# Grouping x loads and output stores of an eight-expert MoE feed-forward, and one buffer size for w2, on one Trainium2 core

## The chip, the cores and the metric

One of the eight cores of a Trainium2 (trn2) chip runs the kernel. The metric is the device time of one execution in microseconds (us); lower is better. The number for a kernel is the median of its runs.

## The reference

```python
def reference(x, w1, w2):
    h = np.matmul(x, w1)
    h = np.maximum(h, 0)
    return np.matmul(h, w2).astype(np.float32)
```

There are 8 experts. x is 8 x 256 x 512, w1 is 8 x 512 x 2048, w2 is 8 x 2048 x 512, the output 8 x 256 x 512, all in fp32 in HBM. Each expert's 256 rows pass through two dense layers with a ReLU between them. The weights are 4 MB per expert and layer, 64 MB in all; x and the output are 0.5 MB per expert.

## The kernel before

The kernel computes in bf16 with fp32 accumulation. Nearly every load converts fp32 to bf16 on the way, in the DMA itself; such loads are issued from POOL (GpSimd), all on one queue (q0 in the profile). Only x of experts 0 and 1 is loaded as fp32 from SP, and cast on VectorE (`load_x_first`, L60 to L64).

Per expert there are three steps. `prepare` (L104) transposes x on TensorE, 8 blocks of 128 x 128, and VectorE copies the result to SBUF. `layer1` (L117) makes the 16 blocks of 128 hidden units, two at a time: 4 matmuls of 128 x 256 for each block (L125), then a ReLU on ScalarE (L132). `layer2` (L139) accumulates two output tiles of 128 x 512 over the 16 rows k of the hidden dimension: 32 matmuls (L148); for experts 6 and 7, whose w2 comes in pieces, with k as the outer loop (L144), so that a piece can be used as it lands. The finished tiles are copied to SBUF (L157, L159).

A "row" of w2 is here one k: 128 partitions x 512 columns, 256 KB read and 128 KB written. A w2 of one piece has 16 rows. `PIECES` (L53) splits expert 6 into 8, 4, 4 and expert 7 into 4, 4, 3, 2, 1, 1, 1 rows, and each size has a buffer pool of its own (`BUFS`, L54; three buffers for the whole w2). w1 has 4 buffers, x in bf16 has 4, the output 5.

The order on TensorE and POOL is written out by hand (L166); the other engines' order follows from the data. `loads` (L89 to L94) holds the loads in their order: for each expert x of the next one, w1, w2; at the end w1 of expert 7 goes ahead of w2 of expert 6. `issue` (L96) takes loads from its front as long as they are allowed at this point of the loop. In the loop over experts (L172) POOL issues loads two to three experts ahead, then the store of the expert before (L175), while TensorE runs layer 1 of expert e, the transposes of e + 1, layer 2 of e. In the last turn layer 1 of expert 7 is put ahead of layer 2 of expert 6 (L178). Experts 4, 5 and 6 (`DEFER`, L56) are stored after all loads (L181). Expert 7's two output tiles are stored by SP and ACT, each as soon as it is copied (L160 to L162).

A load waits on POOL until its buffer is free, and also until the transfer eight places earlier on POOL's queue has landed, since that one's semaphore is used again. Everything behind it in POOL's order waits too.

Of the kernel before, what the change touches and what calls it, by code (L numbers as in the profile page):

```python
# [9 lines left out]
FP32 = mybir.dt.float32  # L10
BF16 = mybir.dt.bfloat16


@with_exitstack
def kernel(
    ctx: ExitStack,
    tc: tile.TileContext,
    x: bass.AP,
    w1: bass.AP,
    w2: bass.AP,  # L20
    out: bass.AP,
):
    nc = tc.nc
    P = 128
    E, C, H = x.shape
    F = w1.shape[2]
    MC = C // P
    K1 = H // P
    K2 = F // P

    x_v = x.rearrange("e (p mo) k -> e p (mo k)", mo=MC)
    out_v = out.rearrange("e (p mo) k -> e p (mo k)", mo=MC)
    w1_v = w1.rearrange("e (p ko) n -> e p (ko n)", ko=K1)
    w2_v = w2.rearrange("e (p j) n -> e p (j n)", p=P)

    const = ctx.enter_context(tc.tile_pool(name="const", bufs=1))
    x_pool = ctx.enter_context(tc.tile_pool(name="x_pool", bufs=2))
    xb_pool = ctx.enter_context(tc.tile_pool(name="xb_pool", bufs=4))  # L40
    xT_pool = ctx.enter_context(tc.tile_pool(name="xT_pool", bufs=2))
    w1_pool = ctx.enter_context(tc.tile_pool(name="w1_pool", bufs=4))
    w2_pool = ctx.enter_context(tc.tile_pool(name="w2_pool", bufs=1))
    hT_pool = ctx.enter_context(tc.tile_pool(name="hT_pool", bufs=2))
    out_pool = ctx.enter_context(tc.tile_pool(name="out_pool", bufs=5))
    psum_t = ctx.enter_context(tc.tile_pool(name="psum_t", bufs=1, space=bass.MemoryType.PSUM))
    psum_h = ctx.enter_context(tc.tile_pool(name="psum_h", bufs=3, space=bass.MemoryType.PSUM))
    psum_o = ctx.enter_context(tc.tile_pool(name="psum_o", bufs=4, space=bass.MemoryType.PSUM))

    identity = const.tile([P, P], BF16, name="identity")  # L50


    PIECES = {E - 2: [8, 4, 4], E - 1: [4, 4, 3, 2, 1, 1, 1]}  # L53
    BUFS = {16: 3, 8: 1, 4: 4, 3: 1, 2: 1, 1: 3}  # L54

    DEFER = (E - 4, E - 3, E - 2)  # L56

    xbs, w1s, w2s, outs = {}, {}, {}, {}

    def load_x_first(e):  # L60
        t = x_pool.tile([P, MC * H], FP32, name="x_sb")
        nc.sync.dma_start(t[:], x_v[e])
        xbs[e] = xb_pool.tile([P, MC, P, K1], BF16, name="xb")
        nc.vector.tensor_copy(xbs[e][:].rearrange("p m q k -> p (m q k)"), t[:])  # L64

    def load_x(e):
        xbs[e] = xb_pool.tile([P, MC, P, K1], BF16, name="xb")
        nc.gpsimd.dma_start(xbs[e][:].rearrange("p m q k -> p (m q k)"), x_v[e])  # L68

    def load_w1(e):  # L70
        w1s[e] = w1_pool.tile([P, K1 * F], BF16, name="w1_sb")
        nc.gpsimd.dma_start(w1s[e][:], w1_v[e])  # L72

    def load_w2(e):
        w2s[e] = []
        k = 0
        for n in PIECES.get(e, [16]):
            c = w2_pool.tile([P, n * H], BF16, name=f"w2_{n}", bufs=BUFS[n])
            nc.gpsimd.dma_start(c[:], w2_v[e, :, k * H:(k + n) * H])  # L79
            for q in range(n):  # L80
                w2s[e].append(c[:, q * H:(q + 1) * H])
            k += n

    def store(e):
        nc.gpsimd.dma_start(out_v[e], outs[e][:].rearrange("p m h -> p (m h)"))  # L85

    loads = []  # L89
    for e in range(E):  # L90
        if e + 1 < E and e >= 1:
            loads.append((load_x, e + 1))
        loads += [(load_w1, e), (load_w2, e)]
    loads[-3], loads[-2] = loads[-2], loads[-3]  # L94

    def issue(upto):  # L96
        while loads:
            f, e = loads[0]
            if (f, e) not in upto:
                break  # L100
            loads.pop(0)
            f(e)

    def prepare(e):  # L104
        xb = xbs[e]
        xt_ps = psum_t.tile([P, K1, MC, P], BF16, name="xt_ps")
        for ko in range(K1):
            for mo in range(MC):
                nc.tensor.transpose(xt_ps[:, ko, mo, :], xb[:, mo, :, ko], identity[:])  # L109
        xT = xT_pool.tile([P, K1, C], BF16, name="xT")  # L110
        nc.vector.tensor_copy(  # L111
            xT[:].rearrange("p k c -> p (k c)"),
            xt_ps[:].rearrange("p k m q -> p (k m q)"),
        )
        return xT

    def layer1(e, xT):  # L117
        w1_r = w1s[e][:].rearrange("p (ko q j) -> p ko q j", ko=K1, j=K2)
        hT = hT_pool.tile([P, K2, C], BF16, name="hT")
        for pr in range(K2 // 2):  # L120
            h_ps = psum_h.tile([P, 2, C], FP32, name="h_ps")
            for s in range(2):
                j = pr * 2 + s
                for ko in range(K1):
                    nc.tensor.matmul(  # L125
                        h_ps[:, s, :],
                        w1_r[:, ko, :, j],
                        xT[:, ko, :],
                        start=(ko == 0),
                        stop=(ko == K1 - 1),  # L130
                    )
            nc.scalar.activation(  # L132
                hT[:, pr * 2:pr * 2 + 2, :].rearrange("p a c -> p (a c)"),
                h_ps[:].rearrange("p a c -> p (a c)"),
                mybir.ActivationFunctionType.Relu,
            )
        return hT

    def layer2(e, hT):  # L139
        last = e == E - 1  # L140
        out_sb = outs[e] = out_pool.tile([P, MC, H], FP32, name="out_sb")
        o_ps = [psum_o.tile([P, H], FP32, name="o_ps") for _ in range(MC)]
        if e in PIECES:
            order = [(k, m) for k in range(K2) for m in range(MC)]  # L144
        else:
            order = [(k, m) for m in range(MC) for k in range(K2)]
        for k, m in order:
            nc.tensor.matmul(  # L148
                o_ps[m][:],
                hT[:, k, m * P:(m + 1) * P],  # L150
                w2s[e][k],
                start=(k == 0),
                stop=(k == K2 - 1),
            )
            if k == K2 - 1:
                if last and m == 1:
                    nc.scalar.copy(out_sb[:, m, :], o_ps[m][:])  # L157
                else:
                    nc.vector.tensor_copy(out_sb[:, m, :], o_ps[m][:])  # L159
                if last:  # L160
                    eng = nc.scalar if m == 1 else nc.sync
                    eng.dma_start(out_v[e, :, m * H:(m + 1) * H], out_sb[:, m, :])  # L162

    load_x_first(0)
    load_x_first(1)
    with tc.manual_schedule(engines={mybir.EngineType.PE, mybir.EngineType.Pool}):  # L166
        f, e = loads.pop(0)
        f(e)
        make_identity(nc, identity)
        issue([(load_w2, 0), (load_x, 2), (load_w1, 1), (load_w2, 1), (load_x, 3), (load_w1, 2)])  # L170
        xT = prepare(0)
        for e in range(E - 1):  # L172
            issue([(load_w2, e + 2), (load_x, e + 4), (load_w1, e + 3), (load_w1, E - 1), (load_w2, e + 1)])
            if e > 0 and e - 1 not in DEFER:
                store(e - 1)  # L175
            hT = layer1(e, xT)
            xT = prepare(e + 1)
            if e == E - 2:  # L178
                hT_last = layer1(E - 1, xT)
            layer2(e, hT)  # L180
        for e in DEFER:  # L181
            store(e)
        layer2(E - 1, hT_last)


# [1 line left out]
_INS = ['x', 'w1', 'w2']  # L187
_OUTS = [((8, 256, 512), 'float32')]
# [25 lines left out]
```

## Time and profile before

| | us |
|---|---|
| median of 8 runs | 184.25 (183.96 to 184.78) |
| the profiled execution | 184.25 |
| its span | 182.5 |
| busy: PE, PEld | 131.6, 92.2 |
| busy: ACT, POOL, DVE | 40.1, 20.8, 17.1 |
| mean granted TensorE clock | 0.931 |

The span is the part of the execution that the trace shows; 1.75 us lie around it. A profile page gives busy time by engine, then the span in 40 slices with a digit for each engine (tenths busy), then the DMA queues, then the chain of work that ended last, then groups of instructions with what ended the idle time before each, and last the DMA issues with the KB written and the time from issue to landing. In the names, `w_sb` is w1, `w` is w2 and `xb` is x in bf16. The trace behind the page can be asked for one line's instructions, for waits, and for any window of time. In a window "DMA share" is the mean busy share of the 16 DMA engines; it can pass 1 because packets overlap.

### The profile page before, as it was taken

To read this page: it belongs to the slowest core of one execution; us is meant where nothing else is said; L and a number is where in the kernel's file an instruction comes from. 1 tells how busy PE (TensorE), PEld (TensorE's weight loads), DVE (VectorE), ACT (ScalarE), POOL (GpSimd) and SP (SyncE) were. 2 spreads that over 40 slices of the span, in tenths; PEclk is the share of its full clock that TensorE was granted. 3 is DMA by queue.
4 is the path that set the end of the run, shared out by engine and by line. 5 is a ranking of instruction groups with operands and counts; after the bars stand their busy time and mean duration, and the time that the engine had idled before them with its cause. 6 is when DMAs were issued, how large, how long until landed. Compare 5 with 4: busy or idle time off the path is not lost.

```text
span 182.5 us, 1871 instructions
## 1 busy us (share of the span) xinstructions
PE 131.6 (72%) x824; PEld 92.2 (51%) x832; DVE 17.1 (9%) x25; ACT 40.1 (22%) x66; POOL 20.8 (11%) x43
## 2 busy tenths in 40 slices
PE   0205999199974999289970999929887498999860
PEld 0104884079423874079430795328732397964320
DVE  1200011100120011100130001200102001001010
ACT  2000450026101440026100252004600064630010
POOL 7401010110201011010200202011020101122200
PEclk9999999969999799969998589996999789999998
DMA  7999999999999999999999999999998999999993
GB/s 257 199 226 215 201 219 226 219 208 192 243 226 201 208 226 226 205 205 209 247 183 259 198 205 240 230 248 215 221 235 190 215 228 260 204 259 228 204 350 140
DMA packets 5911, 40.48 MB, mean 222 GB/s; under 512 B 656, under 2 KB 1040, under 8 KB 3984
## 3 DMA queue, kind: packets, MB, share of 16 engines
q0 software_dynamic: 5328, 38.80, 97.4%
q1 hardware_dynamic: 432, 1.31, 1.9%
q10 hardware_dynamic: 144, 0.26, 0.4%
q8 instruction: 6, 0.10, 0.2%
q14 instruction: 1, 0.01, 0.0%
HBM read 71.30 MB, written 4.19 MB: 414 GB/s over the span
## 4 chain that ended last, share of the span: by engine, by line
DMA 62%; another core or an unknown queue 25%; POOL 4%; PE 3%; issue 3%; ACT 0%; POOLq 0%
DMA w_sb<-in_w_dram 24%; DMA xb<-in_x_dram 24%; DMA w<-in_w_dram 15%; PE o_ps L148 3%; POOL w L79 1%; POOL xb L68 1%; POOL w_sb L72 1%; POOL out_dram L85 1%; ACT out_sb L157 0%; POOL identity masks.py:199 0%; POOL identity masks.py:197 0%; POOLq L79 0%; POOLq L85 0%; POOLq L198 0%
## 5 line engine op out<-in xcount | busy, mean ns | idle before, releaser
L125 PE MATMUL h_ps<-xT,w_sb 128*128 128x256 bf16 x512 | 71.1, 310 | 36.1 <-DMA w_sb<-in_w_dram 35.2
L125 PEld LDWEIGHTS <-w_sb 128*128 128x128 bf16 x512 | 63.3, 150 | 45.4 <-DMA w_sb<-in_w_dram 39.4
L132 ACT ACTIVATE hT<-h_ps 128x512 bf16<-128x512 f32 x64 | 38.2, 597 | 121.6 <-PE h_ps L125 121.6
L148 PE MATMUL o_ps<-w,hT 128*128 128x512 bf16 x248 | 56.6, 379 | 4.2 <-DMA w<-in_w_dram 3.8
L148 PEld LDWEIGHTS <-hT 128*128 128x128 bf16 x256 | 24.9, 98 | 33.7 <-issue 5.5
L79 POOL DMA_DIRECT2D w<-in_w_dram x16 | 8.7, 542 | 63.0 <-DMA w_sb<-in_w_dram 36.6
L159 DVE COPY out_sb<-o_ps 128x512 f32<-128x512 f32 x15 | 10.3, 691 | 58.1 <-PE o_ps L148 58.1
L111 DVE COPY xT<-xt_ps 128x1024 bf16<-128x1024 bf16 x8 | 5.5, 691 | 97.4 <-PE xt_ps L109 97.4
L109 PE MATMUL xt_ps<-identity,xb 128*128 128x128 bf16 x64 | 5.3, 230 | 4.7 <-DVE xb L64 4.7
L72 POOL DMA_DIRECT2D w_sb<-in_w_dram x8 | 4.6, 574 | 31.1 <-DMA w<-in_w_dram 17.8
L85 POOL DMA_DIRECT2D out_dram<-out_sb x7 | 3.8, 537 | 33.8 <-DMA w<-in_w_dram 11.3
L109 PEld LDWEIGHTS <-xb 128*128 128x128 bf16 x64 | 4.7, 117 | 4.7 <-DVE xb L64 4.7
L68 POOL DMA_DIRECT2D xb<-in_x_dram x6 | 3.2, 532 | 22.8 <-DMA w_sb<-in_w_dram 13.4
L157 ACT COPY out_sb<-o_ps 128x512 f32<-128x512 f32 x1 | 0.6, 586 | 14.7 <-PE o_ps L148 14.7
L64 DVE CAST xb<-x_sb 128x1024 bf16<-128x1024 f32 x2 | 1.4, 694 | 4.5 <-DMA x_sb<-in_x_dram 4.5
L132 ACT ACT_TABLE_LOAD x1 | 1.3, 1283 | 0.7 <-PEq L198 0.7
masks.py:199 POOL TENSOR_SCALAR_AFFINE_SELECT identity<-identity 128x128 bf16<-128x128 bf16 x1 | 0.3, 289 | 0.1
masks.py:197 POOL MEMSET identity<- 128x128 bf16 x1 | 0.2, 225 | 0.0
L198 POOL MEMSET const-float32-0.0<- 128x1 f32 x1 | 0.1, 99 | 0.2 <-issue 0.2
L198 POOL MEMSET const-bfloat16-1.0<- 128x1 bf16 x1 | 0.1, 102 | 0.0
L198 POOL MEMSET const-uint8-127<- 128x1 uint8 x1 | 0.1, 102 | 0.0
L198 POOL MEMSET const-float32-1.0<- 128x1 f32 x1 | 0.1, 99 | 0.0
## 6 DMA issues: line engine op xcount, KB each, us to landing
w_sb<-in_w_dram POOLq DMA_DIRECT2D x8, 2048.0 KB, 51.9
w<-in_w_dram POOLq DMA_DIRECT2D x6, 2048.0 KB, 49.0
out_dram<-out_sb POOLq DMA_DIRECT2D x7, 512.0 KB, 32.4
w<-in_w_dram POOLq DMA_DIRECT2D x4, 512.0 KB, 36.8
xb<-in_x_dram POOLq DMA_DIRECT2D x6, 256.0 KB, 45.0
x_sb<-in_x_dram SPq DMA_DIRECT2D x2, 512.0 KB, 3.6
w<-in_w_dram POOLq DMA_DIRECT2D x1, 1024.0 KB, 47.1
w<-in_w_dram POOLq DMA_DIRECT2D x1, 384.0 KB, 18.8
```

The source lines that it names most:

```text
L64: nc.vector.tensor_copy(xbs[e][:].rearrange("p m q k -> p (m q k)"), t[:])
L68: nc.gpsimd.dma_start(xbs[e][:].rearrange("p m q k -> p (m q k)"), x_v[e])
L72: nc.gpsimd.dma_start(w1s[e][:], w1_v[e])
L79: nc.gpsimd.dma_start(c[:], w2_v[e, :, k * H:(k + n) * H])
L85: nc.gpsimd.dma_start(out_v[e], outs[e][:].rearrange("p m h -> p (m h)"))
L109: nc.tensor.transpose(xt_ps[:, ko, mo, :], xb[:, mo, :, ko], identity[:])
L111: nc.vector.tensor_copy(xT[:].rearrange("p k c -> p (k c)"), xt_ps[:].rearrange("p k m q -> p (k m q)"),)
L125: nc.tensor.matmul(h_ps[:, s, :], w1_r[:, ko, :, j], xT[:, ko, :], start=(ko == 0), stop=(ko == K1 - 1),)
L132: nc.scalar.activation(hT[:, pr * 2:pr * 2 + 2, :].rearrange("p a c -> p (a c)"), h_ps[:].rearrange("p a c -> p (a c)"), mybir.ActivationF ...
L148: nc.tensor.matmul(o_ps[m][:], hT[:, k, m * P:(m + 1) * P], w2s[e][k], start=(k == 0), stop=(k == K2 - 1),)
L157: nc.scalar.copy(out_sb[:, m, :], o_ps[m][:])
L159: nc.vector.tensor_copy(out_sb[:, m, :], o_ps[m][:])
```

## The change

- x of experts 2 to 7 is loaded in pairs (2, 3), (4, 5), (6, 7), one DMA each; there are two pair buffers.
- Outputs are stored in groups, one DMA each: (0, 1), (2, 3), and (4, 5, 6) after all loads. Expert 7 is stored as before. Each group has an output tile of its own, so none is used twice.
- w2 has one buffer size, of 16 rows, four of them. Pieces are slices of one such tile: expert 6 in 8, 8 and expert 7 in 4, 4, 4, 2, 2.
- Ahead of the loop the first two loads (w1 and w2 of expert 0) are taken singly, and the identity for the transposes is made twice.

```diff
-    PIECES = {E - 2: [8, 4, 4], E - 1: [4, 4, 3, 2, 1, 1, 1]}
-    BUFS = {16: 3, 8: 1, 4: 4, 3: 1, 2: 1, 1: 3}
-    DEFER = (E - 4, E - 3, E - 2)
+    PIECES = {E - 2: [8, 8], E - 1: [4, 4, 4, 2, 2]}
+    GROUPS = [(0, 1), (2, 3), (4, 5, 6), (7,)]
+    GROUP = {e: g for g in GROUPS for e in g}
+    DEFER = GROUPS[-2]
+    X_GROUPS = [(2, 3), (4, 5), (6, 7)]
...
-    def load_x(e):
-        xbs[e] = xb_pool.tile([P, MC, P, K1], BF16, name="xb")
-        nc.gpsimd.dma_start(xbs[e][:].rearrange("p m q k -> p (m q k)"), x_v[e])
+    def load_x(g):
+        t = xb_pool.tile([P, 2, MC, P, K1], BF16, name="xb2")
+        nc.gpsimd.dma_start(
+            t[:].rearrange("p e m q k -> p e (m q k)"), xg_v[:, g[0]:g[0] + 2, :]
+        )
+        for i, e in enumerate(g):
+            xbs[e] = t[:, i]
...
-        w2s[e] = []
+        w2s[e] = t = w2_pool.tile([P, K2 * H], BF16, name="w2_sb")
         k = 0
-        for n in PIECES.get(e, [16]):
-            c = w2_pool.tile([P, n * H], BF16, name=f"w2_{n}", bufs=BUFS[n])
-            nc.gpsimd.dma_start(c[:], w2_v[e, :, k * H:(k + n) * H])
-            for q in range(n):
-                w2s[e].append(c[:, q * H:(q + 1) * H])
+        for n in PIECES.get(e, [K2]):
+            nc.gpsimd.dma_start(t[:, k * H:(k + n) * H], w2_v[e, :, k * H:(k + n) * H])
             k += n
...
-    def store(e):
-        nc.gpsimd.dma_start(out_v[e], outs[e][:].rearrange("p m h -> p (m h)"))
+    def store(g):
+        nc.gpsimd.dma_start(
+            og_v[:, g[0]:g[-1] + 1, :], outs[g][:].rearrange("p e m h -> p e (m h)")
+        )
...
         f, e = loads.pop(0)
         f(e)
         make_identity(nc, identity)
-        issue([(load_w2, 0), (load_x, 2), (load_w1, 1), (load_w2, 1), (load_x, 3), (load_w1, 2)])
+        f, e = loads.pop(0)
+        f(e)
+        make_identity(nc, identity)
+        issue([(load_w2, 0), (load_x, X_GROUPS[0]), (load_w1, 1), (load_w2, 1), (load_w1, 2)])
         xT = prepare(0)
         for e in range(E - 1):
-            issue([(load_w2, e + 2), (load_x, e + 4), (load_w1, e + 3), (load_w1, E - 1), (load_w2, e + 1)])
-            if e > 0 and e - 1 not in DEFER:
-                store(e - 1)
+            issue(
+                [(load_w2, e + 2), (load_w1, e + 3), (load_w1, E - 1), (load_w2, e + 1)]
+                + [(load_x, g) for g in X_GROUPS if g[0] <= e + 4]
+            )
+            for g in GROUPS[:-2]:
+                if g[-1] == e - 1:
+                    store(g)
...
-        for e in DEFER:
-            store(e)
+        store(DEFER)
         layer2(E - 1, hT_last)
```

`xg_v` and `og_v` are x and out seen as "p e (mo k)": for each partition, the experts, and for each expert 4 KB.

## The prediction

> **What bounds the kernel now.** I first read the page's part 2 (slices) and part 3 (queues), then the landings of single transfers, then the chain of waits, and last the final 12 us in short windows.
>
> ```profile
> PE 131.6 (72%) x824; PEld 92.2 (51%) x832; DVE 17.1 (9%) x25; ACT 40.1 (22%) x66; POOL 20.8 (11%) x43
> ...
> DMA  7999999999999999999999999999998999999993
> ...
> q0 software_dynamic: 5328, 38.80, 97.4%
> ...
> HBM read 71.30 MB, written 4.19 MB: 414 GB/s over the span
> ```
>
> TensorE is busy 72% of the span, but the DMA row is 9 in all slices except the first, one in the middle and the last, and POOL's queue q0 alone fills 97.4%. The kernel is a stream of bytes. The wait list says the same: layer 1 waits 35.2 us for w1.
>
> Next, whether that stream ever runs dry. POOL issues each transfer long before it lands:
>
> ```profile
> w_sb<-in_w_dram POOLq DMA_DIRECT2D x8, 2048.0 KB, 51.9
> w<-in_w_dram POOLq DMA_DIRECT2D x6, 2048.0 KB, 49.0
> out_dram<-out_sb POOLq DMA_DIRECT2D x7, 512.0 KB, 32.4
> ```
>
> The last number is us from issue to landing; the KB are those written (bf16), so a weight load reads 4 MB. With some 50 us between issue and landing there are always several transfers queued, and POOL's own waits, most of them for the landing of the transfer eight places earlier, cost nothing.
>
> Adding issue and time to landing for single transfers gives the pace: w1 of expert 2 lands at 57.4, w2 of expert 2 at 67.1, x of expert 4 at 68.3, w1 of expert 3 at 78.0. So 9.7 us for a full weight, 1.25 for a 0.5 MB x. One place is out of line: w1 of expert 4 lands at 100.2, 11.3 us after x of expert 5 (88.9), with the DMA share at 1.01 in 88 to 101. The page does not say why.
>
> The end is the chain's last part, and the windows (length, busy us of PE, PEld, DVE, ACT, POOL, clock, DMA share, GB/s):
>
> ```profile
> 144.18 26.60 DMA w<-in_w_dram
> 170.78 0.04 issue
> 170.82 1.89 PE o_ps L148 x8
> 172.71 0.01 issue
> 172.72 0.81 PE o_ps L148 x3
> 173.52 0.05 issue
> 173.57 2.32 PE o_ps L148 x10
> 175.90 0.04 issue
> 175.94 0.61 PE o_ps L148 x2
> 176.54 0.02 issue
> 176.57 0.59 ACT out_sb L157
> ```
>
> ```profile
> 176.00:177.00 1.00, 0.53 (x2) 0.04 (x1) 0.65 (x1) 0.43 (x1) 0.00 (x0) 1.00 1.06 434
> 177.00:178.00 1.00, 0.00 (x0) 0.00 (x0) 0.04 (x1) 0.15 (x1) 0.00 (x0) 1.00 0.58 234
> 178.00:179.00 1.00, 0.00 (x0) 0.00 (x0) 0.00 (x0) 0.00 (x0) 0.00 (x0) 1.00 1.03 397
> ```
>
> The pieces of the last w2 land at 168.3, 170.8, 172.7, 173.9, 174.6, 175.1, 175.9. The last two matmuls run right after, the copies, and the two final stores are issued at 177.07 (SP) and 177.18 (ACT). Behind the last piece in q0 are the three deferred stores, landing at 177.2, 178.4, 179.7; the final stores land at 180.3 and 181.0, that is 0.6 and 1.3 later. Each is 256 KB, 0.6 at the stream's pace, so on the slowest of the 16 DMA engines they stood behind the deferred stores. At 177 to 178 the DMA share is 0.58: other engines were already empty. So bytes set the end, with the chain of matmul, copy and store close behind.
>
> **What the Trainium skill says.** "DMA: Bandwidth & Descriptors", section "Anatomy of one DMA", gives a transfer a fixed 2.0 us, mostly completion latency, and says that DMA engines wait on no semaphore, the issuing sequencer does. The trace agrees with the second. The first is latency, not occupancy: one-row pieces land 0.5 to 0.8 us apart. "Rules for kernel authors" of the same page advises one large transfer for many small ones, and counts those under 64 KB as mostly overhead; the smallest here writes 128 KB, and the last five pieces together lie 5% above the pace (below), so this trace leaves little to win.
>
> **The change part by part**, against the profiled execution (184.25 us, span 182.5, 1.75 around it; the runs' median is also 184.25).
>
> *Bytes.* None removed: weights, x and outputs are the same. With a stream that never dries, only the cost per transfer and the two ends can change.
>
> *Fewer transfers.* q0 goes from 37 to 27: x 6 to 3, stores 7 to 3, pieces of w2 10 to 7. What one costs beyond its bytes: a full weight has 16 rows in 9.7 us, 0.606 a row. The last five pieces of the last w2 (3, 2, 1, 1, 1: 8 rows) took 175.9 - 170.8 = 5.1 against 4.85, so 0.05 each. An x or a store is worth two rows, 1.21, and took 1.25 to 1.29: 0.04 to 0.08 each. What is not shown is whether this belongs to the transfer or to its 128 rows. For the pieces both go, so 3 x 0.05 = 0.15 is saved in either case. For the seven merged x and stores the rows stay: between 0 and 7 x 0.08 = 0.55. I take 0.04 each, 0.28. Sum 0.43, bounds 0.15 and 0.7. All of it lies in the one stream, so it counts in full as long as the stream sets the end.
>
> *Shape.* The grouped x and stores step over experts inside one transfer. No transfer of that shape is in this trace; they are 3 x 2.5, 2 x 2.5 and 3.8, some 16 us. The descriptor's run per expert is the same 4 KB of fp32, so I price it at nothing, from -0.2 to +0.8 (5% of 16).
>
> *The last pieces: 4, 4, 4, 2, 2.* Matmuls go at 7.07 / 31 = 0.23 each. Before, the last piece freed two; now four. From the second piece's landing T1: before, the third piece landed at T1 + 1.9, and PE, hardly idle since, ended at T1 + 5.76. After, the third piece has four rows and lands at T1 + 2.45; 16 matmuls from there end at T1 + 2.45 + 3.67 + about 0.1 = T1 + 6.2. So the final stores are issued about 0.45 later relative to T1, T1 itself 0.2 earlier. Is it covered? The last piece lands at T1 + 4.95, three stores follow in 3.7 to 3.8, the final ones in 1.25: T1 + 9.95. By the chain: issue at T1 + 6.75 (SP) and 6.85 (ACT); a first transfer on the idle SP queue at the start took about 3.2 from issue for 512 KB, so 2.0 beyond its 1.2; the ACT store then ends near T1 + 6.85 + 2.0 + 0.6, or + 1.2 behind SP's: 9.45 to 10.05. The bytes still last as long or longer. I take 0; without cover it costs 0.45.
>
> *Deferred stores as one.* It waits for the copies of expert 6. Before, the first of the three went at 166.5; those copies end at 169.2, so the one is issued there. Nothing but POOL's end is queued behind it, and the engines reach it only after the last piece (175.7). Over 5 us of cover: 0.
>
> *Second identity, w2 of expert 0 issued singly.* 0.23 + 0.29 on POOL, with a wait perhaps 0.6, ahead of the next issues. w1 of expert 0 is in flight until 15.8, so the queue stays full; the transposes at 4.69 wait for the cast of x anyway. 0.
>
> *Buffers.* With four whole w2 buffers, w2 of expert e waits for layer 2 of e - 4; before, three buffers, and none for the last two. With two pair buffers for x, the pair (6, 7) waits for the transposes of expert 3, and behind that stand w1 of expert 5 and the first grouped store. Those transposes follow layer 1 of expert 2, which starts at about 58 and lasts 7.2: issue near 66, and by the sum of bytes the pair's turn comes at about 108. Cover 40 us. The first piece of the last w2 waits for layer 2 of expert 3, near 96, turn at 166. Stores now go in pairs, later in order, but the bytes ahead of the last w2 are the same. If a cover were gone, the stream would stand for the difference.
>
> Sum: 184.25 - 0.43 = 183.8.
>
> **The rivals.**
> A: the fixed cost belongs to the rows. Then merging x and stores saves nothing, 0.15 remains: 184.1. For it: an x's 0.04 beyond its bytes is as well explained by its small rows as by being one transfer.
> B, slower: the chain from the last piece overtakes the bytes. Place: after the last w2 piece; price: two more matmuls, 0.45; from the point where the final stores' data comes later than the slowest engine's end of the deferred stores, a margin of 0.5 at best, and none by the upper estimate above. With no saving in the stream: 184.7. For it: the 0.58 at 177 to 178; against it: the final stores landing in step after the third deferred one.
> C, slower: the two-level shape runs 5% below pace: +0.8 - 0.4, so 184.65. It decides from 2.6% on. Nothing in the profile speaks for it.
> D: the 1.5 us lost at 88 to 101 depends on which transfers are then in flight, and is partly shed: 183.2. The after kernel moves other transfers there, but nothing ties the loss to them.
>
> **How the numbers follow.** 0.2% of 184.25 is 0.37, about what a measurement of this kernel can tell from no change. Forecast 183.8 (own range 183.5 to 184.1): 0.50, of which 0.12 stays within 0.37. A 0.22, within. B 0.12, C 0.06, slower. D 0.10, faster. So faster 0.48, same 0.34, slower 0.18. The range goes from 183.2, where D lies, to 184.7, where B lies; more than that needs two mishaps.
>
> **What would show it.** Right: q0 near 97%, ten transfers fewer, weights still 9.7 us apart, merged x at 2.45 rather than 2.5, the last piece's landing 0.3 earlier, final stores landing 0.6 and 1.2 after the grouped store. B shows as an end of the grouped store well before the ACT store's landing, by over 1.3. C shows as an x pair above 2.6 us. Wrong altogether: a slice in mid-span with the DMA digit below 9, or matmuls of expert 7 waiting for all five pieces.

## The result and the profile after

The changed kernel takes 183.23 us (median of 11 runs) against 184.25 (32 runs). The ratio is 0.9944, 95% interval 0.9933 to 0.9956: 1.0 us faster, with the interval at 0.8 to 1.2. The forecast was 183.8, in the range of 183.2 to 184.7. So the direction was right, and the gain 2.4 times the forecast's 0.43: the time lies inside the range by 0.03 us, at the end where rival D stood, and outside the forecast's own narrower range of 183.5 to 184.1.

The profiled execution took 183.25 us, its span 181.2. First the page: busy time, the DMA row of the 40 slices, POOL's queue and the HBM line.

```profile
PE 126.6 (70%) x824; PEld 89.7 (50%) x832; DVE 17.2 (9%) x25; ACT 40.1 (22%) x66; POOL 17.1 (9%) x35
...
DMA  6999999999999999999999999999999999999994
...
q0 software_dynamic: 4784, 38.80, 97.6%
...
HBM read 71.30 MB, written 4.19 MB: 417 GB/s over the span
```

The same bytes go through the same queue, and no slice between the first and the last is below 9: still a stream that never runs dry. Packets fell from 5328 to 4784. The issues (KB written, median us from issue to landing) show that coarser transfers also put more bytes in the queue ahead:

```profile
w_sb<-in_w_dram POOLq DMA_DIRECT2D x14, 2048.0 KB, 62.1
out_dram<-out_sb POOLq DMA_DIRECT2D x2, 1024.0 KB, 55.5
...
xb<-in_x_dram POOLq DMA_DIRECT2D x3, 512.0 KB, 45.0
```

The one long new wait on POOL is that of the last x pair for the transposes of expert 3 (POOL's timeline: start, length, idle before and what ended it):

```profile
65.61 0.71 POOL L74 DMA_DIRECT2D xb<-in_x_dram  x1 [26.91 <-PE xt_ps L119]
```

It is issued at 65.6 and lands at 110.6. For 27 us POOL stood still with everything behind that wait, and the DMA row shows nothing of it.

The end, first as the chain of waits, then in windows of 1 us (the last two numbers are DMA share and GB/s):

```profile
134.07 38.67 DMA w_sb<-in_w_dram
172.74 0.04 issue
172.78 0.81 PE o_ps L161 x3
173.59 0.05 issue
173.64 2.77 PE o_ps L161 x12
176.41 0.02 issue
176.43 0.59 ACT out_sb L170
```

```profile
177.00:178.00 1.00, 0.00 (x0) 0.00 (x0) 0.00 (x0) 0.02 (x1) 0.00 (x0) 1.00 0.52 211
178.00:179.00 1.00, 0.00 (x0) 0.00 (x0) 0.00 (x0) 0.00 (x0) 0.00 (x0) 1.00 1.02 391
```

The last five pieces land at 167.9, 170.3, 172.7, 174.0 and 175.3, the group of three stores at 179.05, the final stores at 179.7 and 180.3. These are again 0.6 and 1.3 behind the deferred stores, so here too the bytes on the slowest DMA engine set the end.

The last store lands 0.6 us earlier than before (180.9 to 180.3), but the span is 1.3 shorter (182.5 to 181.2). Another 0.65 us therefore lies behind the last store, in the program's end inside the span. Outside the span it grew, from 1.75 to 2.05 us, so that 0.4 remain. SP's wait list shows the part inside. In each line: who waits at which line of the kernel for whom, us in total, times, longest. First the kernel before, then the one after:

```profile
SPq L209 <- PEq L209: 1.3, 2, 1.0
```

```profile
SPq L226 <- PEq L226: 0.6, 2, 0.5
```

These are the meetings of all engines at the end of the program. In the trace it is POOL that comes late: from the start of its last clearing of semaphores to the start of its next instruction it took 0.5 us before and 0.15 after.

### The profile page after: what moved, and what is told of

It is laid out like the page before. It is cut to its first block, busy times and chain, and to the rows that moved or that the text cites. A ratio compares the mean times of both kernels' runs of the same rounds, so it can differ in the third digit from the quotient of the medians.

```text
span 181.2 us, 1855 instructions
## 1 busy us (share of the span) xinstructions
PE 126.6 (70%) x824; PEld 89.7 (50%) x832; DVE 17.2 (9%) x25; ACT 40.1 (22%) x66; POOL 17.1 (9%) x35
## 3 DMA queue, kind: packets, MB, share of 16 engines
q0 software_dynamic: 4784, 38.80, 97.6%
## 4 chain that ended last, share of the span: by engine, by line
DMA 65%; PE 16%; another core or an unknown queue 13%; POOL 2%; issue 2%; ACT 0%; POOLq 0%
DMA w_sb<-in_w_dram 40%; DMA xb<-in_x_dram 25%; PE h_ps L135 9%; PE o_ps L161 6%; POOL w_sb L88 1%; PE xt_ps L119 1%; POOL out_dram L92 0%; POOL xb L74 0%; POOL w_sb L82 0%; ACT out_sb L170 0%; POOL identity masks.py:199 0%; POOL identity masks.py:197 0%; POOLq masks.py:199 0%; POOLq L88 0%
## 5 line engine op out<-in xcount | busy, mean ns | idle before, releaser
L135 PE MATMUL h_ps<-xT,w_sb 128*128 128x256 bf16 x512 | 66.5, 298 | 36.6 <-DMA w_sb<-in_w_dram 36.6
L135 PEld LDWEIGHTS <-w_sb 128*128 128x128 bf16 x512 | 60.7, 148 | 43.8 <-DMA w_sb<-in_w_dram 39.9
L161 PE MATMUL o_ps<-w_sb,hT 128*128 128x512 bf16 x248 | 56.4, 379 | 8.4 <-DMA w_sb<-in_w_dram 8.0
L88 POOL DMA_DIRECT2D w_sb<-in_w_dram x13 | 7.0, 536 | 77.9 <-DMA w_sb<-in_w_dram 74.8
L82 POOL DMA_DIRECT2D w_sb<-in_w_dram x8 | 4.7, 587 | 29.8 <-DMA w_sb<-in_w_dram 17.1
L74 POOL DMA_DIRECT2D xb<-in_x_dram x3 | 2.2, 718 | 26.9 <-PE xt_ps L119 26.9
L92 POOL DMA_DIRECT2D out_dram<-out_sb x3 | 2.2, 728 | 17.4 <-DVE out_sb L172 14.8
```

The costliest lines, as they stand in the source:

```text
L74: nc.gpsimd.dma_start(t[:].rearrange("p e m q k -> p e (m q k)"), xg_v[:, g[0]:g[0] + 2, :])
L88: nc.gpsimd.dma_start(t[:, k * H:(k + n) * H], w2_v[e, :, k * H:(k + n) * H])
L92: nc.gpsimd.dma_start(og_v[:, g[0]:g[-1] + 1, :], outs[g][:].rearrange("p e m h -> p e (m h)"))
L135: nc.tensor.matmul(h_ps[:, s, :], w1_r[:, ko, :, j], xT[:, ko, :], start=(ko == 0), stop=(ko == K1 - 1),)
L161: nc.tensor.matmul(o_ps[m][:], hT[:, k, m * P:(m + 1) * P], w2s[e][:, k * H:(k + 1) * H], start=(k == 0), stop=(k == K2 - 1),)
```

## The experiments

Two theories were set against each other: S, that the whole gain lies in the stream as a cost per transfer on POOL's queue (1.0 us over ten transfers); and T, that part of it lies in the program's end and comes from POOL's shorter instruction list.

All ratios are to the kernel before, measured beside the run on the same chip. Its own median there was 184.16 for the first four of the runs below "after", 184.08 for the next four and 184.02 for the last four, so the ratios are to be compared, not the medians. "List" counts all instructions of POOL in the trace, those of its sequencer included. The last three columns are of the one profiled execution: landing of the last store, us from there to the end of the span, and to the end of the execution. That last one is the execution's time less the landing, so what lies ahead of the span is in it too.

| kernel | median us | ratio (95%) | list | last store | to span's end | to the end |
|---|---|---|---|---|---|---|
| before | 184.25 | 1 | 71 | 180.9 | 1.55 | 3.3 |
| after | 183.23 | 0.9944 (0.9933 to 0.9956) | 59 | 180.3 | 0.9 | 2.9 |
| x in pairs alone | 183.82 | 0.9987 (0.9976 to 0.9997) | 67 | 180.9 | 0.9 | 3.0 |
| grouped stores alone | 183.56 | 0.9972 (0.9959 to 0.9985) | 65 | 180.2 | 0.9 | 2.9 |
| w2 pieces alone | 183.65 | 0.9975 (0.9968 to 0.9981) | 70 | 180.7 | 1.3 | 3.05 |
| after, 12 fillers | 183.53 | 0.9971 (0.9961 to 0.9981) | 71 | 180.4 | 1.4 | 3.2 |
| before, short list | 183.99 | 0.9999 (0.9982 to 1.0016) | 68 | 180.5 | 1.0 | 3.3 |
| after, again | 183.08 | 0.9945 (0.9923 to 0.9967) | 59 | 180.8 | 0.9 | 2.9 |
| after, weights cut by columns | 183.73 | 0.9977 (0.9965 to 0.9989) | 73 | 180.2 | 1.7 | 3.5 |
| after, weights cut by partitions | 184.77 | 1.0030 (1.0012 to 1.0047) | 73 | 181.1 | 1.7 | 3.5 |
| after, one identity | 182.88 | 0.9939 (0.9927 to 0.9950) | 55 | 180.3 | 0.9 | 2.7 |
| after, 24 fillers | 183.07 | 0.9948 (0.9936 to 0.9960) | 83 | 180.5 | 0.9 | 2.7 |
| after, last w2 in 4, 4, 4, 4 | 182.89 | 0.9937 (0.9925 to 0.9949) | 58 | 179.9 | 0.9 | 2.7 |
| after, last w2 in seven pieces | 183.40 | 0.9964 (0.9951 to 0.9976) | 61 | 180.5 | 0.9 | 2.9 |

### One part at a time

The kernel before with x in pairs alone; with grouped stores alone; with the one w2 buffer size and the coarser pieces alone. Each is that part of the diff above. With the stores, two sizes were cut to make room for the group tiles:

```diff
-    xb_pool = ctx.enter_context(tc.tile_pool(name="xb_pool", bufs=4))
+    xb_pool = ctx.enter_context(tc.tile_pool(name="xb_pool", bufs=3))
...
+            outs[g] = out_pool.tile([P, max(len(g), 2), MC, H], FP32, name=f"out_sb{g[0] % 7}")
```

x in pairs:


> The kernel before with x loaded in pairs alone: three transfers fewer on POOL, same bytes. Theory S (the whole gain lies in the stream, a fixed cost per transfer on POOL's queue, 1.0 us over ten transfers): 0.3 us faster than before, and an x pair lands 2.4 us after the transfer ahead of it, against 2.5 for two single ones. Theory T (about 0.65 us of the gain lies behind the last store's landing, in the program's end on POOL, which has 12 instructions fewer in the changed kernel; merging itself saves under 0.03 each): within 0.2 us of before unless POOL's shorter list already removes the late end; the pair lands 2.5 after.

Grouped stores:


> The kernel before with grouped stores alone: four transfers fewer on POOL (x in bf16 has three buffers in place of four, to make room, and the last output tile shares its buffer with the first group). Theory S: 0.4 us faster. Theory T: within 0.2 us, or 0.65 faster if POOL's list is now short enough; the group of three stores lands 3.75 us after the last piece of w2, as three single stores did (3.8).

Pieces:


> The kernel before with the one buffer size and the coarser pieces of w2 alone: three transfers fewer on POOL, and four matmuls in place of two behind the last piece. Theory S: 0.3 us faster. My forecast's sum: 0.15 faster, with the last piece landing about 0.2 earlier after the second piece (4.95 against 5.1). Theory T: the same 0.15, or 0.65 more if POOL's list is now short enough. If the chain behind the last piece decided, it would be up to 0.3 slower.

Measured: 0.24, 0.52 and 0.46 us faster by the ratios. The landings say how much of each is the stream. Three x pairs land 2.46 to 2.52 behind the transfer ahead of them, single ones mostly 1.25 each: nothing to 0.05 for each merge. The group of three stores took 3.8 (175.1 to 178.9), three single ones 3.8. Only the pieces are cheaper in sum: the 16 rows of the last w2 took 9.97 us before, from the landing ahead of them, and 9.82 in five pieces; those of expert 6 went from 9.76 to 9.73. Against this, what lies behind the last store shrank by 0.25 to 0.45 in all three. For x in pairs that is the whole gain, since its last store lands where it did before; S did not foresee this. With grouped stores the last store also lands 0.7 us earlier, but not by the merge: the weight directly ahead of the first store landed 10.4 us after the transfer ahead of it, in place of 11.3 before (see the last section), and this profiled execution was the fastest of its six runs. In the run with pieces alone the longest of SP's last waits is 0.8, between the other two; its list is one instruction shorter than before.

### POOL's list

Twelve one-column memsets are put behind POOL's last store, where POOL has 10 us without work:

```diff
         store(DEFER)
+        for _ in range(12):
+            nc.gpsimd.memset(filler[:], 0.0)
```

> The changed kernel with 12 one-column memsets on POOL after its last store, where POOL has 10 us without work, so that its instruction list is as long as before. Theory S: 183.2, as the changed kernel. Theory T: the late end comes back, 0.5 to 0.7 us slower than the changed kernel, 183.8, with the time from the last store's landing to the end of the span at 1.5 us in place of 0.9.

The late end is back. SP's last waits in this run:

```profile
SPq L229 <- PEq L229: 1.1, 2, 1.0
```

The ratio is 0.9971 against 0.9944 and 0.9945 of the changed kernel, 0.5 us slower by the ratios, 0.3 by the medians, with not a byte or a transfer changed. The last store landed at 180.4, as in the changed kernel (180.3). T foresaw this, with somewhat more (0.5 to 0.7); S has no place for it.

The reverse: the kernel before, with instructions of POOL taken away (seven x buffers, and the memset of the identity on VectorE). The expectation counts four; the trace has three fewer.

```diff
-    xb_pool = ctx.enter_context(tc.tile_pool(name="xb_pool", bufs=4))
+    xb_pool = ctx.enter_context(tc.tile_pool(name="xb_pool", bufs=7))
...
-        make_identity(nc, identity)
+        nc.vector.memset(identity[:], 0.0)
+        make_identity(nc, identity, nomemset=True)
```

> The kernel before with every transfer as it is, but four instructions fewer on POOL: the identity's memset goes to VectorE, and x in bf16 has seven buffers, so that three waits go. POOL's list is then as long as in the run with x in pairs, which had no late end. Theory T: the last store lands as before, the program's end takes 0.75 us after SP's last wait in place of 1.4, and the kernel is 0.3 to 0.65 us faster than before, with no transfer merged. Theory S: 184.2, as before.

T's number failed here: the ratio is 0.9999. SP's last waits:

```profile
SPq L210 <- PEq L210: 0.8, 2, 0.5
```

The wait inside the span did shrink (0.8 in total against 1.3), and the span ends 1.0 us after the last store in place of 1.55. But 2.3 us of the execution lie outside the span, where it was 1.75 before, and the last semaphore event that the trace holds comes 0.5 us later behind the span's end than before (2.4 against 1.9). The delay has only moved behind the span. So the span alone misleads: the last column of the table, which counts to the end of the execution, is the one to read.

Twice as many fillers, and fewer instructions than the changed kernel has (its identity made once, the memset on VectorE):

```diff
-        for _ in range(12):
+        for _ in range(24):
```

> The changed kernel with 24 one-column memsets on POOL after its last store. The list is 12 longer than in the kernel before. If the end's cost depends on where the list ends in blocks that are fetched, it is between the changed kernel and the cut by columns: 183.1 to 183.8, with 2.9 to 3.5 us behind the last store's landing; if it grows with the list, 3.7 or more, 184.0.

```diff
-        make_identity(nc, identity)
+        nc.vector.memset(identity[:], 0.0)
+        make_identity(nc, identity, nomemset=True)
         f, e = loads.pop(0)
         f(e)
-        make_identity(nc, identity)
```

> The changed kernel with the identity made once, and its memset on VectorE: POOL's list shorter by another three instructions. If what the end costs falls with every instruction, it is 0.1 us faster than the changed kernel; if there is only a point that the list must not pass, as the runs so far say, it is the same, 183.1 to 183.2, with 2.9 us from the last store's landing to the end of the execution.

With 24 fillers, a longer list than any other, the late end is gone again; SP's last waits:

```profile
SPq L229 <- PEq L229: 0.6, 2, 0.5
```

So the cost does not grow with the list. The single identity is the same as the changed kernel within the intervals, with 2.7 us at the end in place of 2.9: whether every instruction counts a little is left open.

From the last store to the end it took 2.7 us with lists of 55, 58 and 83, 2.9 with 59, 61 and 65, 3.0 with 67, and 3.05 to 3.5 with 68 to 73. It depends on where the list ends, and the traces show the place. In all five profiles with 70 to 73 instructions POOL pauses once after the last store, for 0.4 us, and each time directly ahead of its 69th instruction. With 70 in the list this is the last but one, with 71 (before, and the 12 fillers) the third from the end, with 73 the fifth. Lists of up to 68 do not reach that place inside the span; with 68, in the kernel before with the short list, 0.5 us came behind the span. With 83 the 69th instruction is a filler at 173.6, long before the last store, and no pause stands ahead of it. Apart from that place, POOL is also late at the first meeting in some runs, by 0.2 us in the kernel before and 0.3 in the two cuts.

A packet of 8 KB on an instruction queue goes along with this. None comes near the end with lists of 55 to 61; with 65 to 73 one comes 1.7 to 2.7 us after the last store; with 83 it comes 7.5 us before it, when POOL has nothing to do. This looks like a fetch of instructions in blocks. But the packet starts 0.7 us after the pause has ended, and the changed kernel has 0.3 us more outside its span than the run with one identity (2.05 against 1.8), with no such packet in either. The place in the list is shown; the mechanism is not.

### Price of a transfer

Every full weight load of the changed kernel in two, by columns and by partitions:

```diff
-        nc.gpsimd.dma_start(w1s[e][:], w1_v[e])
+        n = K1 * F // 2
+        for k in (0, n):
+            nc.gpsimd.dma_start(w1s[e][:, k:k + n], w1_v[e, :, k:k + n])
...
-        for n in PIECES.get(e, [K2]):
+        for n in PIECES.get(e, [8, 8]):
```

> The changed kernel with every full weight load cut in two by columns: 14 transfers more on POOL, and twice the descriptors for the same bytes. POOL's list is then long enough for the late end (0.3 to 0.5 us by theory T). Stream by my forecast's price of 0.05 for a transfer with its rows: + 0.7, so 184.2 to 184.5 with the late end. Theory S, with 0.1 a transfer: + 1.4 and no late end, 184.6. If a transfer costs 0.02: 183.2 + 0.3 + 0.4 = 183.9.

```diff
-        nc.gpsimd.dma_start(w1s[e][:], w1_v[e])
+        for k in (0, 64):
+            nc.gpsimd.dma_start(w1s[e][k:k + 64], w1_v[e, k:k + 64])
...
+        if e not in PIECES:
+            for k in (0, 64):
+                nc.gpsimd.dma_start(t[k:k + 64], w2_v[e, k:k + 64])
+            return
```

> The changed kernel with every full weight load cut in two by partitions (64 and 64): 14 transfers more, but the same number of rows and descriptors. If the cost belongs to the transfer, it is as slow as the cut by columns; if it belongs to the rows, only the late end on POOL remains, 183.6 to 183.8. If halves of the partitions use the engines worse, it is slower than the cut by columns, and a weight's pair lands over 10 us after the one ahead.

Fourteen transfers more by columns: 183.73, below all three numbers expected for it. By the times alone a transfer would cost nothing, since the end explains what was lost against the changed kernel (3.5 against 2.9). The landings say otherwise. The table has the median gap between a transfer's landing and that of the one ahead, over all fourteen profiles; the very first transfer, the one directly ahead of the first store and the halves by partitions are left out. A "partition row" is the stretch of memory that a transfer moves for one partition and one expert: 128 in most transfers, 256 in a pair.

| transfer | KB in HBM | partition rows | us |
|---|---|---|---|
| w2 piece, one row | 256 | 128 | 0.65 |
| w2 piece, two rows | 512 | 128 | 1.25 |
| x or store, single | 512 | 128 | 1.26 |
| w2 piece, three rows | 768 | 128 | 1.88 |
| w2 piece, four rows | 1024 | 128 | 2.45 |
| x pair | 1024 | 256 | 2.49 |
| store pair | 1024 | 256 | 2.51 |
| three stores | 1536 | 384 | 3.76 |
| half a weight, by columns | 2048 | 128 | 4.87 |
| whole weight | 4096 | 128 | 9.69 |

All ten lie within 0.03 us of 0.602 for each 256 KB and 0.048 for each 128 partition rows. Two halves by columns take 9.73, a whole weight 9.69. So a transfer together with its 128 partition rows does cost the forecast's 0.05, and the 14 further ones about 0.65 in the stream. They do not show in the time because something else fell away: the weight ahead of the first store landed 10.2 us after the transfer ahead of it, in place of 11.0 in the changed kernel. S, which asked for 0.1 on every transfer, is out.

One warning on reading such sums. Every transfer ends with 16 events in the trace, one for each DMA engine, and the landing given here is the last of them; the delays of that slowest engine hide small prices. From the landing of x (4, 5) to that of x (6, 7) it took 41.4 us with eight weight halves (69.8 to 111.2) and 41.4 with four whole weights (69.2 to 110.6), as if the cut were free. Taken by the first of the 16 events it took 41.42 with halves, and 41.21 to 41.27 in the seven profiles with whole weights.

The cut by partitions was slower by a further 1.0 us (184.77), of which the end explains nothing. Its runs spread over 183.8 to 185.75. Its last piece landed at 176.0, 0.9 later than with the cut by columns, but only on the slower engines: the first of the 16 events is at 173.4 in both. Of the third expectation the first half came true; the weight's pairs landed 9.8 to 10.6 us after the one ahead, not all over 10. Why the slower engines fall behind was not followed up. So this run cannot tell whether the price belongs to the transfer or to the partition rows.

### The last pieces

```diff
-    PIECES = {E - 2: [8, 8], E - 1: [4, 4, 4, 2, 2]}
+    PIECES = {E - 2: [8, 8], E - 1: [4, 4, 4, 4]}
```

> The changed kernel with the last w2 in 4, 4, 4, 4: eight matmuls in place of four behind the last piece, 0.9 us more on the chain piece, matmuls, copy, store. If the deferred group of stores covers it on the slowest DMA engine (my forecast gave the cover as up to 0.5): the final stores land 0.0 to 0.9 later. Full cover: 183.1; no cover: 184.0; by the forecast's cover after the change, a few tenths are seen, 183.3 to 183.6.

Covered: 182.89, the ratio 0.9937, no slower than the changed kernel. The chain of waits of this run:

```profile
174.77 0.04 issue
174.81 1.90 PE o_ps L161 x8
176.71 0.02 issue
176.73 0.58 ACT out_sb L170
```

From the last piece to the end of the matmuls it is now 1.9 us, where the changed kernel had 1.1. The final stores land at 179.3 and 179.95, 0.8 and 1.45 after the group at 178.5, so 0.2 us of the chain has come out from behind the bytes. The cover is near its end.

```diff
-    PIECES = {E - 2: [8, 8], E - 1: [4, 4, 4, 2, 2]}
+    PIECES = {E - 2: [8, 8], E - 1: [4, 4, 3, 2, 1, 1, 1]}
```

> The changed kernel with the last w2 in 4, 4, 3, 2, 1, 1, 1 as before. By the landings' sums the fine pieces cost 0.11 in the stream: 183.2 to 183.3, and the chain behind the last piece is 0.45 shorter without use. If the pieces are the change's main part, 183.5.

183.40, the ratio 0.9964, about 0.3 us slower than the changed kernel and with the same 2.9 at the end. Fine pieces do cost in the stream: the last w2 took 9.91 to 9.97 us in the five profiles with seven pieces, 9.81 to 9.89 in the eight with five. The ratios give more than this 0.1.

### Once more

> The changed kernel once more, on the chip of the runs beside it: 183.2 by both theories, and a second profile that shows whether the long packets of all engines at 116 us, and the first weight's late landing on one engine in the kernel before, come again at the same place.

183.08. Its profiled execution was the slowest of its eight runs, 183.73, and there the first weight landed on the last engine at 16.2, against 15.0 in the first profile of the same kernel and 15.8 in that of before. That landing varied over 15.0 to 16.4 in all the profiles, whatever the kernel. So the 0.75 us by which it came earlier in the first profile of after is not of the change. The long packets came again at the same place, 115 to 119 us (up to 2.2 us in place of 1.23 for a packet of a weight), but they cost less: the weight there, directly ahead of the first store, landed 10.2 us after the transfer ahead of it, against 11.0 in the first profile.

## Why the prediction was right, and where its sum was wrong

**What bounds it.** Right. The DMA row, q0 at 97.6% and the final stores 0.6 and 1.3 behind the group are as forecast.

**Fewer transfers: the price.** The price itself was right: 0.05 for a transfer with its 128 partition rows, by all landings. For the pieces, where both go, 0.15 was forecast; the landings give 0.11 for the last w2 and 0.06 for that of expert 6, so 0.17. The merged x and stores were mis-sized: 0.28 forecast, measured about 0.1 together in the stream. Rival A had this term nearly right, and the landings fit a price on partition rows. A price on the transfer would fit as well if the two-level shape (rival C) took it back, and no run separates the two. One reading was off: the landings of the one-row pieces were rounded, and they lie 0.65 to 0.71 us apart, not 0.5 to 0.8; the sum of five pieces is not touched. What the Trainium skill says on this ("DMA: Bandwidth & Descriptors", "Anatomy of one DMA": a fixed 2.0 us that is mostly completion latency) fits: with one-row pieces 0.65 us apart, the full queue hides that latency.

**Sum, and what was left out of it.** The sum counted the 1.75 us around the span, and all that lies behind the last store, as fixed. That is the step that failed. This stretch went from 3.3 to 2.9 us, and the fillers gave 0.25 of it back. It is as large as the whole forecast, and needs none of the mechanisms that the forecast weighed. That the time still fell into the range, at its edge, was luck.

**The account.** Of 1.0 us: 0.4 behind the last store (profiles; 0.3 to 0.5 by the fillers' run), 0.2 to 0.3 in the stream by the sums of landings, and perhaps 0.3 ahead of the first store, where a weight took 11.3 us before and 11.0 after (rival D, below). The rest is not assigned, and the last part is not secure. The interval of the ratio is worth 0.2 either way, and the slowest DMA engine's lag differs by more than that between executions of one kernel: at the last piece it stood 1.95 us behind the fastest engine in the first profile of the changed kernel, 2.4 in the second. The pieces, by their two experiments, are worth 0.2 to 0.35 rather than 0.17. The three parts, run alone, add up to 1.2 by the ratios, with the shorter list counted up to three times.

**Shape** (rival C). No pair came near the sign of 2.6 us; it costs what two singles cost, 2.49 to 2.52 in this profile. The sign for a gain, 2.45, did not come either.

**The last pieces** (rival B). Right with its cover: relative to the landing of the second piece (170.3), the last piece came at 5.0 (forecast 4.95), SP's store was issued at 6.65 (6.75), and the last store landed at 10.0 (9.95). The cover was put at 0.5 at best; eight matmuls in the last piece show about 0.7 of their 0.9 hidden.

**Deferred group.** Issued at 168.7, landing behind the pieces, no cost, as forecast. **Buffers.** The pair's issue at 65.6 (forecast 66), its landing at 110.6 (turn forecast at 108), no cost. **Second identity.** No cost in the stream; but its instructions stand in POOL's list, and the run with one identity is the same within the intervals (0.9939 against 0.9944).

**Rival D.** In part, perhaps. The stretch was not shed in the changed kernel, it moved with the first store and lost 1.3 us in place of 1.6 over a weight's usual 9.7. The last section has the numbers of the other runs.

No version beats the changed kernel by more than the intervals; the last w2 in four equal pieces (0.9937) and the single identity (0.9939) come first.

## What to carry to other kernels

In a queue that is never empty, merging transfers gained almost nothing here where the number of partition rows stayed: two x loads took 2.52 us, a pair 2.49. Count bytes and partition rows, and look for the rest of the gain at the two ends. A price of some hundredths of a us is read from the medians of many landings, not from the sum of one stretch, which the slowest engine decides. Time from the last landing to the end of the execution, not to the end of the span, belongs into the comparison of two kernels, since a change in POOL's instruction count moved it here by some tenths of a us either way. Before giving credit to one mechanism, change the instruction count alone with instructions that do nothing.

## What was not expected of the hardware

The end of a program, from the last store's landing to the end of the execution, took 2.7 to 3.5 us, depending on POOL's instruction list, and not in step with its length: 83 instructions in the trace were as cheap as 55, and 68 to 73 the dearest, with a pause of 0.4 us always ahead of the 69th.

Bytes and partition rows alone give the pace of the queue: 0.602 us for each 256 KB and 0.048 for each 128 partition rows, within 0.03 us for transfers of 256 KB to 4 MB (fitted to the landings of the fourteen profiles).

The 1.5 us lost in mid-span in the kernel before goes with the first store on the queue: in every profile it is the weight directly ahead of that store which is late. Where that store comes early (the kernel before, also with the short list, with x in pairs or with pieces alone), the weight directly ahead of it is w1 of expert 4; it landed 10.6 to 11.3 us after the transfer ahead of it, in place of 9.7, at about 100 us. Where it comes later, and the weights are whole (eight profiles: the changed kernel twice, the fillers, grouped stores alone and three more), it was w1 of expert 5, with 10.2 to 11.0 us, at about 121. By the first of the 16 events it was 10.4 to 10.5 in the early group and 10.0 to 10.4 in the late one. So a later first store may lose some 0.3 us less; the groups overlap, and two executions of the changed kernel differ by 0.8 (11.0 and 10.2). No later store shows it. Some 20 packets of that weight are long within 3 to 4 us (up to 2.8 us in place of 1.23, at 94 to 98 before and 115 to 119 after), that is before the store's own turn. What in the first store does this, or whether it does, was not tried.
